# A hybrid convolution and RWKV-7 block: the gate's adaLN rows spread over block 0, the state's update by additions, and split projection weights kept in DRAM

## The chip, the core and the metric

The kernel runs on one core of a Trainium2 chip. The metric is device microseconds (us) from start to end of one execution. Before the change the median of three runs is 3080.32 us (3077.19 to 3084.64).

## What is computed

One decoder block over 2048 tokens of width 1024 with two parallel token mixers and a final RMSNorm. The reference, cut to what matters here:

```python
mod = einsum('bd,de->be', silu(c), ada_w[l]) + ada_b[l]
shift, scale, gate = split(mod, 3, axis=-1)
h = rmsnorm(x, norm_g[l]) * (1 + scale[:, None, :]) + shift[:, None, :]
p = einsum('bsd,de->bse', h, w_in[l])
c_val, c_gate, c_og, ts, r_og, g_conv, g_rwkv = split(p, SPLITS, axis=-1)
y_conv = conv_branch(c_val, c_gate, c_og, ...)      # GLU, causal depthwise conv of width 31, LayerNorm, swish, @ w_conv_out
y_rwkv = rwkv7_branch(ts, r_og, ...)                # 16 heads of 64, per-head norm, SiLU gate, @ w_rwkv_out
m = sigmoid(g_conv) * y_conv + sigmoid(g_rwkv) * y_rwkv
x = x + gate[:, None, :] * (m @ w_out[l])
return rmsnorm(x, final_g)

# in rwkv7_branch, the scan over tokens, per head:
sk = einsum('bhvk,bhk->bhv', state, kk_t)
state = state * w_t[:, :, None, :] - sk[..., None] * b_t[:, :, None, :] + v_t[..., None] * k_t[:, :, None, :]
o_t = einsum('bhvk,bhk->bhv', state, r_t)
```

## The kernel before

**Layout.** Features stand on the 128 partitions, tokens along a row. The tokens are cut into four blocks of 512 (`NB`, `TB`). A matrix product is made of three products of split values, so that it keeps the accuracy of float32: every operand is split in a high part (a cast to `fp32r` on ACT) and a low part (a subtraction). `load_w` brings a 128-column tile of weights (512 KB), casts it on ACT (L175), subtracts on DVE or POOL (L177), and for the input projections writes both parts to DRAM (L181, L182) so that later blocks read them back ready (L168, L169). All weight tiles (`w_st`, `w_hi`, `w_lo`) share six buffers (`WB`): a tile that is loaded and split takes three of them, one that is read back takes two. `mm3` (L192) is a projection: 24 matmuls of 512 columns, or 48 of 256, into a PSUM buffer `ps_main`, of which there are two.

**First phase, blocks 0 to 3** (loop at L859). `hprep` makes the normalised input `h`; in block 0 it also computes shift and scale from 16 of the 24 adaLN rows (`ada_steps`). Then four groups of two pairs of heads. `pair` projects r, k and v, makes the decay factors (`pe` is the decay over a chunk of 64 tokens, one value per feature and chunk), the matrices `KR` and `BK`, the masked products `As` (from copies of `BK` by ACT, `BKz`, L518) and, by eight transposes on PE (L555) and two copies (L556), `tk`, the transposed `BK`. `group` then inverts the triangular blocks of `As` (out to DRAM as `dA`, L595; back as `La`, L600; 62 steps on POOL, L609 and L611; out and back again) and walks through 8 chunks in a chain (L659 to L685): matmuls of `KR` with the state `S`, an addition (L670), matmuls with `As`, a multiplication to `uv` (L675), matmuls of `tk` with `uv`, and the update of the state on DVE, for each of the four heads `S = xo * pe + Se` (L683), where ACT made `Se = S * pe` (L665). `pe` thus multiplies both parts of the new state, chunk by chunk.

Beside the chain PE has input projections to do: those of `conv` (with the 31-tap convolution on DVE, L761) and of `gates`. A tile scheduler puts all of it into one order per engine ahead of time; the order is fixed when the program runs. All DMAs are issued by SP, one after another in its order; a DMA that waits for its data or for a free buffer holds those behind it.

**Rows of the gate.** Behind group 0 of block 0 (L890 to L896) the last eight adaLN rows are read, 512 KB each, in four pairs (`ada_cols`, L206) into buffers of tag `As`, and each is multiplied with the condition's row `srow` and summed on DVE. The result, half the gate, goes to `grow_d` in DRAM. In block 1 `ogate` (L147) multiplies w_o by it, in 16 halves of a tile: load, multiply on POOL, cast on ACT (L157), subtract on POOL (L158), and store both parts (L160). The last phase reads them back.

**Last phase** (from L964, 2446 us in the profile). For each block `rproj` (w_ro) and `cproj` (w_co) project the two mixers' outputs and evict them with the sigmoid gates to `mr` (L962 and L949); the sum is split and goes through w_o (L1059 to L1061); `finish` makes the final RMSNorm of 128 tokens: a few steps on 128x1 (L1074 to L1077 with the reciprocal square root, L125 to L130), two multiplications (L1080) and the stores. In this phase each block loads and splits w_ro and w_co anew, 8 tiles of each: 64 casts (L175) and 64 subtractions on DVE (L177). While one block's w_o is multiplied, the next block's inputs are prepared: `osplit` (L927) and `lnorm` (L984, LayerNorm over the convolution's channels, with `pmean`, `pvar` and `prl` on PE).

## Time and profile before

| what | value |
|---|---|
| time, median of 3 runs | 3080.32 us |
| the profiled execution: its own time | 3079.25 us |
| its span, first to last instruction | 3077.6 us |
| mean granted clock of TensorE | 0.977 |
| PE busy | 2918.8 us, 95% (25672 matmuls) |
| PEld busy (weight loads of PE, beside matmuls) | 2759.5 us, 90% |
| DVE busy | 2182.2 us, 71% |
| POOL busy | 1161.0 us, 38% |
| ACT busy | 1059.7 us, 34% |
| DMA | 638.41 MB, mean 207 GB/s |

Engines: PE is TensorE (PEld its weight loads), DVE VectorE, ACT ScalarE, POOL GpSimd, SP SyncE, which issues the DMAs. A row names the line of the code, the engine, the operation, the tile written and the tiles read. A row of waits gives the time in which the first engine stood idle before that work and what ended the wait. The stages, by where the tiles of each block begin to move: block 0 from 0 to 655 us, block 1 to 1240, block 2 to 1825, block 3 to 2446, the last phase to the end.

### The profile page before, as it was taken

Reading aid. Unit: us, or ns where it says so; the run is one execution under the profiler, and the core shown is the slowest. Engines: PE = TensorE matmul, PEld = TensorE weight load, DVE = VectorE, ACT = ScalarE, POOL = GpSimd, SP = SyncE. Lnnn points to the kernel's source line nnn. Section 1 sums busy time; section 2 is a strip of 40 time slices with the busy share of each in tenths; the row PEclk is TensorE's granted clock in tenths of the full one; section 3 lists DMA queues with packets and bytes.
Section 4 is the critical chain, followed back from the end, with each engine's and each line's share of the span. In section 5 each row is a group of like instructions: output and inputs, shape, how many; then the busy total and the mean of one; then the engine's idle time right before and its main releaser. Section 6 shows DMA issues by size and latency. Waiting matters only on the chain.

```text
span 3077.6 us, 64859 instructions
## 1 busy us (share of the span) xinstructions
PE 2918.8 (95%) x25672; PEld 2759.5 (90%) x25672; DVE 2182.2 (71%) x4199; ACT 1059.7 (34%) x1919; POOL 1161.0 (38%) x1724
## 2 busy tenths in 40 slices
PE   6799998999999999999999999999989999699998
PEld 5789998999999999999999998999989888487888
DVE  7677877787777667777768586867699465877553
ACT  4424444343324241424232323233342224343421
POOL 3355554534343434241323326345445016533100
PEclk9989999999999999999999999999989999799999
DMA  8675767664757586555646567647448658766554
GB/s 301 221 239 192 262 206 268 229 235 136 249 160 229 163 269 218 178 167 173 204 149 217 181 202 247 192 142 224 139 146 263 207 187 287 246 205 220 198 182 161
DMA packets 343327, 638.41 MB, mean 207 GB/s; under 512 B 133424, under 2 KB 152176, under 8 KB 343024
## 3 DMA queue, kind: packets, MB, share of 16 engines
q1 hardware_dynamic: 343024, 634.27, 62.8%
q8 instruction: 202, 3.31, 0.4%
q14 instruction: 101, 0.83, 0.1%
HBM read 462.10 MB, written 170.92 MB: 206 GB/s over the span
## 4 chain that ended last, share of the span: by engine, by line
PE 62%; DVE 12%; DMA 10%; POOL 7%; issue 3%; ACT 2%; SPq 2%; DVEq 0%; POOLq 0%; ACTq 0%
PE ps_main L192 43%; PE aux L524 3%; DVE acc L761 2%; DMA w_st<-w_in_t 2%; POOL TT L611 2%; POOL itmp L609 2%; PE xo L673 2%; PE pout L1061 2%; PE pout L1060 2%; PE pout L1059 2%; DMA w_lo<-kl_in 1%; PE xo L668 1%; DMA w_gr<-grow_d 1%; PE xo L679 1%; PE late L695 1%
## 5 line engine op out<-in xcount | busy, mean ns | idle before, releaser
L192 PE MATMUL ps_main<-h_hi,w_hi 128*128 128x256 f32 x4608 | 961.4, 286 | 20.4 <-ACT w_hi L175 12.2
L192 PE MATMUL ps_main<-h_hi,w_lo 128*128 128x256 f32 x4608 | 962.3, 286 | 13.6 <-POOL w_lo L177 8.0
L192 PE MATMUL ps_main<-h_lo,w_hi 128*128 128x256 f32 x4608 | 956.7, 285 | 0.0
L192 PEld LDWEIGHTS ps_main<-h_hi,w_hi 128*128 128x128 f32 x4608 | 721.7, 190 | 30.4 <-ACT w_hi L175 13.3
L192 PEld LDWEIGHTS ps_main<-h_hi,w_lo 128*128 128x128 f32 x4608 | 719.7, 190 | 21.6 <-POOL w_lo L177 10.0
L192 PEld LDWEIGHTS ps_main<-h_lo,w_hi 128*128 128x128 f32 x4608 | 719.8, 190 | 5.2 <-issue 0.5
L761 DVE SCALAR_TENSOR_TENSOR acc<-u,ck,acc 128x512 f32<-128x512 f32 x928 | 698.6, 753 | 20.0
L175 ACT CAST w_hi<-w_st 128x1024 fp32r<-128x1024 f32 x135 | 141.5, 1048 | 368.9 <-DMA w_st<-w_in_t 151.6
L683 DVE SCALAR_TENSOR_TENSOR S<-xo,pe,Se 64x64 f32<-64x64 f32 x512 | 144.6, 282 | 128.1 <-PE xo L679 118.1
L609 POOL TENSOR_TENSOR itmp<-La,TT 128x126 f32<-128x126 f32 (+22 forms) x496 | 180.7, 364 | 141.9 <-DMA La<-dA 105.9
L611 POOL TENSOR_TENSOR TT<-TT,itmp 128x126 f32<-128x126 f32 (+22 forms) x496 | 190.5, 384 | 37.2
L177 DVE TENSOR_TENSOR w_lo<-w_st,w_hi 128x1024 fp32r<-128x1024 f32 x88 | 119.5, 1359 | 103.7 <-ACT w_hi L175 47.7
L177 POOL TENSOR_TENSOR w_lo<-w_st,w_hi 128x1024 fp32r<-128x1024 f32 x47 | 113.5, 2414 | 134.5 <-ACT w_hi L175 109.0
L665 ACT ACTIVATE Se<-S,pe 128x128 f32<-128x128 f32 x256 | 89.0, 395 | 209.1 <-DVE S L683 208.0
L524 PE MATMUL aux<-KR,BKz 128*128 128x128 f32 x1024 | 138.5, 285 | 13.5 <-ACT BKz L518 8.7
L547 POOL TENSOR_TENSOR vv<-rk,vv 128x512 f32<-128x512 f32 x32 | 44.0, 1374 | 284.2 <-ACT rk L546 268.8
L524 PEld LDWEIGHTS aux<-KR,BKz 128*128 128x128 f32 x1024 | 127.6, 198 | 16.1 <-ACT BKz L518 9.1
L675 DVE TENSOR_TENSOR uv<-xo,rn 64x256 f32<-64x256 f32 x128 | 53.7, 420 | 99.8 <-PE xo L673 98.2
L741 ACT ACTIVATE th<-ps_main 128x512 f32<-128x512 f32 x64 | 38.1, 595 | 210.5 <-PE ps_main L192 157.6
L526 DVE TENSOR_TENSOR As<-aux,maskA 128x512 f32<-128x512 f32 x128 | 87.0, 688 | 27.9 <-PE aux L524 26.4
L451 POOL TENSOR_TENSOR wlo<-wf,wl 64x128 fp32r<-64x128 f32 x64 | 37.4, 584 | 173.6 <-ACT wl L448 171.1
L773 ACT ACTIVATE th<-ps_main 128x512 f32<-128x512 f32 x64 | 38.2, 597 | 184.3 <-PE ps_main L192 179.7
(298 smaller groups left out, 5489.0 us busy)
## 6 DMA issues: line engine op xcount, KB each, us to landing
w_hi<-kh_in SPq DMA_DIRECT2D x219, 512.0 KB, 4.0
w_lo<-kl_in SPq DMA_DIRECT2D x219, 512.0 KB, 5.1
w_st<-w_in_t SPq DMA_DIRECT2D x73, 512.0 KB, 5.0
kh_in<-w_hi SPq DMA_DIRECT2D x71, 512.0 KB, 2.9
kl_in<-w_lo SPq DMA_DIRECT2D x71, 512.0 KB, 4.4
w_st<-w_ro_t SPq DMA_DIRECT2D x32, 512.0 KB, 4.0
w_st<-w_co_t SPq DMA_DIRECT2D x32, 512.0 KB, 3.6
w_hi<-kh_o SPq DMA_DIRECT2D x32, 512.0 KB, 3.7
```

Source lines behind the costliest of these rows:

```text
L175: nc.scalar.copy(hi, st)
L177: lo_eng.tensor_tensor(out=lo, in0=st, in1=hi.bitcast(F32), op=ALU.subtract)
L192: nc.tensor.matmul(ps[:, qs], ww[:, k, :], aa[k][:, qs], start=(k == 0 and t == 0 and q == 0), stop=(k == KT - 1 and t == 2 and q == ms - ...
L524: nc.tensor.matmul(pA[:, c // 2, es], BKz[:, hh, c // 2, es], KR[:, cc, es], start=(c == 0), stop=(c == 3), skip_group_check=True)
L526: nc.vector.tensor_tensor(out=Asb[:, hh, c4 * 4:c4 * 4 + 4, :].rearrange("p (a e) n -> p a (e n)", e=2), in0=pA, in1=flat(maskA).unsqueeze ...
L609: nc.gpsimd.tensor_tensor(out=tmp[:, :ni, :nt], in0=La[:, j:j + 1, j + 1:].broadcast_to([P, ni, nt]), in1=TT[:, :ni, j:j + 1].broadcast_to ...
L611: nc.gpsimd.tensor_tensor(out=TT[:, :ni, j + 1:], in0=TT[:, :ni, j + 1:], in1=tmp[:, :ni, :nt], op=ALU.add)
L665: nc.scalar.mul(Se[:, q, :], Sg[:, q, :], R[q]["pe"][:, c:c + 1])
L673: nc.tensor.matmul(xo[pr_, q, hs], As[q][pr_, hh, c, kcol(e)], XO[pr_, c, q, hs], start=(q == 0 and hh == 0), stop=(q == 1 and hh == 1), s ...
L683: nc.vector.scalar_tensor_tensor(out=Sg[hs, q, hs], in0=xo[hs, 2 + q, hs], scalar=R[q]["pe"][hs, c:c + 1], in1=Se[hs, q, hs], op0=ALU.mult ...
L761: nc.vector.scalar_tensor_tensor(out=acc if i + 1 < HALO else yj, in0=u[:, i:i + TB], scalar=ck[:, j, i:i + 1], in1=acc, op0=ALU.mult, op1 ...
L1059: nc.tensor.matmul(o_, mhi[kk][:, ts_], whi[:, k, :], start=first, stop=False, skip_group_check=True)
```

## The change

Four edits.

1. The condition's row `srow` is stored in DRAM once (`srow_d`). Behind each of block 0's four groups a copy of it is read back to all partitions (512 KB) into a buffer of tag `As`, and one pair of adaLN rows (two of 512 KB) is read and multiplied. The gate's column and `grow_d` are finished behind group 3.
2. `BK` is multiplied by `pe` on POOL (32 times, 128x1024), ahead of the transposes that make `tk`. The state's update is then `S = xo + Se`: two additions for a chunk, each over both pairs of one half of the partitions, where there were four operations.
3. `keep` works in block 2: per group four tiles of w_ro or w_co, in two halves each, are loaded, cast on ACT, subtracted on POOL and stored in DRAM, 32 halves in all (32 casts, 32 subtractions, 64 stores of 256 KB).
4. `load_w` finds these in `kept`, so the last phase reads high and low parts back and splits nothing: 64 casts and 64 subtractions are gone there, and two tiles of 512 KB are read where there was one.

```diff
+    srow_d = dp.tile([D], F32, name="srow_d", tag="srow_d")
...
+    pending = [(name, n) for name in ("ro", "co") for n in range(KT)]
+
+    def keep(name, n, half):
+        back = kept.setdefault((name, n), [dp.tile([P, KT, P], F32R, name=f"k{p_}_{name}{n}", tag=f"k{p_}_{name}{n}")
+                                           for p_ in "hl"])
+        hs = slice(half * 4, half * 4 + 4)
+        st, hi, lo = hx("w_st"), hx("w_hi"), hx("w_lo")
+        nc.sync.dma_start(st.rearrange("p (k n) -> p k n", k=4), wsrc[name][n][:, hs, :])
+        nc.scalar.copy(hi.bitcast(F32R), st)
+        nc.gpsimd.tensor_tensor(out=lo.bitcast(F32R), in0=st, in1=hi, op=ALU.subtract)
+        for d_, s_ in zip(back, (hi, lo)):
+            nc.sync.dma_start(d_[:, hs, :].bitcast(F32), s_.rearrange("p (k n) -> p k n", k=4))
...
+        BKe = BK.rearrange("p a (e n) -> p (a e) n", e=2)
+        nc.gpsimd.tensor_tensor(out=BKe, in0=BKe, in1=pe.unsqueeze(2).broadcast_to([P, NCH, 2 * CH]), op=ALU.mult)
         tk = l3.tile([P, NCH, P], F32, name="tk", tag="tk", bufs=TKB)
...
-            for q, hh in heads:
+            for hh in range(2):
                 hs = slice(64 * hh, 64 * hh + 64)
-                nc.vector.scalar_tensor_tensor(out=Sg[hs, q, hs], in0=xo[hs, 2 + q, hs],
-                                               scalar=R[q]["pe"][hs, c:c + 1], in1=Se[hs, q, hs],
-                                               op0=ALU.mult, op1=ALU.add)
+                nc.vector.tensor_tensor(out=Sg[hs, :, hs], in0=xo[hs, 2:4, hs], in1=Se[hs, :, hs], op=ALU.add)
...
+    nc.sync.dma_start(srow_d.unsqueeze(0), srow[0:1])
...
+            if b == 2:
+                for _ in range(4):
+                    n_ = pending.pop(0)
+                    for half in range(2):
+                        keep(*n_, half)
...
-            if b == 0 and g == GG:
-                for _ in ada_cols(srow, l3, "As", ASB, [((16 + k, 17 + k), (hgate_col[:, k:k + 1], hgate_col[:, k + 1:k + 2]))
-                                                        for k in range(0, KT, 2)]):
+            if b == 0:
+                sr = l3.tile([P, 2, D], F32, name="srow2", tag="As", bufs=ASB)[:, 0, :]
+                nc.sync.dma_start(sr, srow_d.unsqueeze(0).broadcast_to([P, D]))
+                for _ in ada_cols(sr, l3, "As", ASB, [((16 + k, 17 + k), (hgate_col[:, k:k + 1], hgate_col[:, k + 1:k + 2]))
+                                                      for k in (2 * g,)]):
                     pass
...
+                if g == 3:
+                    nc.vector.tensor_tensor(out=hgate_col, in0=hgate_col, in1=ab[:, 16:24], op=ALU.add)
...
+                    nc.sync.dma_start(grow_d.rearrange("(n p) -> p n", p=P), hgate_col)
```

The scheduler makes a new order of it. In the rows below the numbers behind names are buffer numbers, and an "x4" at the end of a row stands for so many such instructions in a row. New line numbers run ahead of the old ones: L225 after is L211 before, L186 is L172, L195 and L196 are L181 and L182, L611 is L595, L616 is L600, L562 is L548, L182 and L183 are L168 and L169.

First, SP behind group 0 of block 0, where the adaLN rows (`ada_st`) are issued among the inverse's transfers (`dA`, `La`) and the next weights (`w_st`). Before:

```order
L211 DMA ada_st<-ada_t 128x1024 x4
L181 DMA kh_in_2025<-w_hi 128x1024
L172 DMA w_st<-w_in_t 128x1024
L211 DMA ada_st<-ada_t 128x1024
L595 DMA dA<-As 32x4x32 x7
L548 DMA bv_d_1_100<-vv 128x512
L595 DMA dA<-As 32x4x32
L211 DMA ada_st<-ada_t 128x1024 x3
L744 DMA co_d_0_195<-th 128x512
L600 DMA La<-dA 64x1024 x2
L774 DMA gr_d_0_259<-th 128x512
L182 DMA kl_in_2026<-w_lo 128x1024
```

And after:

```order
L186 DMA w_st<-w_in_t 128x1024
L196 DMA kl_in_1936<-w_lo 128x1024
L913 DMA srow_1859<-srow_d 128x1024
L225 DMA ada_st<-ada_t 128x1024 x2
L195 DMA kh_in_1997<-w_hi 128x1024
L611 DMA dA<-As 32x4x32 x8
L562 DMA bv_d_1_100<-vv 128x512
L758 DMA co_d_0_195<-th 128x512
L616 DMA La<-dA 64x1024 x2
L196 DMA kl_in_1998<-w_lo 128x1024
L186 DMA w_st<-w_in_t 128x1024
L788 DMA gr_d_0_259<-th 128x512
```

A weight load that stood behind four rows stands ahead of `srow_d` and the two rows now, and the second one behind `La`.

Second, SP in block 2 behind its last group's pairs, where that group's inverse begins. Before:

```order
L595 DMA dA<-As 32x4x32 x8
L548 DMA bv_d_7_122<-vv 128x512
L168 DMA w_hi<-kh_in_7845 128x1024
L600 DMA La<-dA 64x1024 x2
L169 DMA w_lo<-kl_in_7846 128x1024
L168 DMA w_hi<-kh_in_7907 128x1024
L169 DMA w_lo<-kl_in_7908 128x1024
```

And after, where `kh_co` and `kl_co` are the stores of `keep`:

```order
L611 DMA dA<-As 32x4x32
L182 DMA w_hi<-kh_in_7799 128x1024
L183 DMA w_lo<-kl_in_7800 128x1024
L616 DMA La<-dA 64x1024
L174 DMA kh_co_21810<-w_hi 128x512
L170 DMA w_st<-w_co_t 128x512
L174 DMA kl_co_21811<-w_lo 128x512
L616 DMA La<-dA 64x1024
L182 DMA w_hi<-kh_in_7861 128x1024
L183 DMA w_lo<-kl_in_7862 128x1024
L174 DMA kh_co_21810<-w_hi 128x512
L170 DMA w_st<-w_co_t 128x512
```

Loads and stores of `keep` now stand between the two halves of `La` and between the weights read back; in groups 0 and 1 they come in bunches of eight halves, and the last sixteen together here.

Third, DVE in the last phase between block 0's output projection and block 1's first projection, where the final RMSNorm of block 0 meets the eviction of block 1's first PSUM buffer to `mr`. Before:

```order
L1080 SCALAR_TENSOR_TENSOR xt_31907<-xt_31907,rs_32399,fg 128x512
L1080 SCALAR_TENSOR_TENSOR xt_31909<-xt_31909,rs_32399,fg 128x512
L1075 TENSOR_SCALAR vs<-vs 128x1
L130 SCALAR_TENSOR_TENSOR rs_32418<-rs_t,rs_32418 128x1
L1074 TENSOR_REDUCE vs<-sq_31923 128x1
L177 TENSOR_TENSOR w_lo<-w_st,w_hi 128x1024
L202 SCALAR_TENSOR_TENSOR y_31741<-th,y_31741 128x512
L962 SCALAR_TENSOR_TENSOR mr_32472<-rth,ps_main 128x512
```

And after (L1104, L1099, L131, L1098, L986 are L1080, L1075, L130, L1074, L962 of before):

```order
L1104 SCALAR_TENSOR_TENSOR xt_31981<-xt_31981,rs_32473,fg 128x512
L1104 SCALAR_TENSOR_TENSOR xt_31983<-xt_31983,rs_32473,fg 128x512
L1099 TENSOR_SCALAR vs<-vs 128x1
L131 SCALAR_TENSOR_TENSOR rs_32492<-rs_t,rs_32492 128x1
L1098 TENSOR_REDUCE vs<-sq_31997 128x1
L126 TENSOR_SCALAR rs_32511<-vs 128x1
L1104 SCALAR_TENSOR_TENSOR xt_31985<-xt_31985,rs_32492,fg 128x512
L1104 SCALAR_TENSOR_TENSOR xt_31987<-xt_31987,rs_32492,fg 128x512
L1099 TENSOR_SCALAR vs<-vs 128x1
L129 TENSOR_TENSOR rs_t<-rs_32511 128x1
L986 SCALAR_TENSOR_TENSOR mr_32546<-rth,ps_main 128x512
```

The subtraction of a weight (L177) and the LayerNorm's L202 no longer stand ahead of `mr`; the second norm's multiplications do.

More of the change, by code (lines that the diff above doesn't have):

```diff
@@ L889, in hybrid_block @@
             group(b, g, h, lora, fill)
-            if b == 0 and g == GG:
-                for _ in ada_cols(srow, l3, "As", ASB, [((16 + k, 17 + k), (hgate_col[:, k:k + 1], hgate_col[:, k + 1:k + 2]))
-                                                        for k in range(0, KT, 2)]):
-                    pass
-                nc.vector.tensor_tensor(out=hgate_col, in0=hgate_col, in1=ab[:, 16:24], op=ALU.add)
-                nc.vector.tensor_scalar(out=hgate_col, in0=hgate_col, scalar1=0.5, scalar2=None, op0=ALU.mult)
-                nc.sync.dma_start(grow_d.rearrange("(n p) -> p n", p=P), hgate_col)
+            if b == 0:
[3 more added lines that the diff above has]
+                                                      for k in (2 * g,)]):
+                    pass
+                if g == 3:
+                    nc.vector.tensor_tensor(out=hgate_col, in0=hgate_col, in1=ab[:, 16:24], op=ALU.add)
+                    nc.vector.tensor_scalar(out=hgate_col, in0=hgate_col, scalar1=0.5, scalar2=None, op0=ALU.mult)
+                    nc.sync.dma_start(grow_d.rearrange("(n p) -> p n", p=P), hgate_col)
             wcount[0] = WDVE
```

## The prediction

> **What bounds the kernel now.** I read the page first, then the busy time of each engine by stage, then what TensorE (PE) waits for, and last the timeline around its longest waits. These are rows of the busy times by stage; the columns are the stretch, its length, PE busy, PEld, DVE, ACT, POOL, the granted clock, DMA share and GB/s.
>
> ```profile
> 0.00:40.00 40.00, 16.51 (x111) 14.87 (x112) 32.83 (x96) 16.61 (x31) 11.76 (x23) 1.00 0.98 375
> 105.00:200.00 95.00, 83.27 (x710) 80.76 (x709) 60.40 (x92) 26.69 (x39) 47.15 (x82) 0.91 0.73 230
> 200.00:655.00 455.00, 434.80 (x4138) 420.11 (x4138) 348.08 (x642) 180.28 (x303) 229.31 (x304) 0.97 0.69 231
> 655.00:1240.00 585.00, 574.81 (x5625) 558.18 (x5624) 427.68 (x861) 196.75 (x381) 221.51 (x396) 1.00 0.65 207
> 1240.00:1825.00 585.00, 580.65 (x5668) 564.93 (x5666) 424.76 (x866) 193.90 (x372) 183.98 (x365) 1.00 0.56 181
> 2240.00:2320.00 80.00, 71.48 (x625) 67.33 (x624) 76.07 (x133) 32.35 (x55) 38.16 (x34) 0.87 0.48 151
> 2560.00:2700.00 140.00, 105.67 (x532) 88.11 (x533) 101.23 (x157) 51.25 (x92) 91.04 (x64) 0.84 0.75 252
> 2700.00:2900.00 200.00, 191.83 (x1058) 163.66 (x1058) 147.65 (x245) 83.02 (x139) 59.05 (x38) 0.99 0.64 212
> ```
>
> PE does nearly all the time's work: in blocks 1 and 2 (655 to 1825) it idles 10.2 and 4.35 us of 585 each. No part of the change removes a matmul, so time can come only out of PE's idle time and out of slow matmuls after it. The stretch that has both is 2560 to 2700, where the last phase goes from block 0's output projection to block 1's projections: 140 - 105.67 = 34.3 us idle at a clock of 0.84. The start of the kernel is the other. Who ended the idle time in that stretch (us in total, times, longest):
>
> ```profile
> PE ps_main L192 <- DVE rs L125: 10.8, 1, 10.8
> PE ps_main L192 <- ACT w_hi L175: 10.8, 2, 6.2
> PE ps_main L192 <- DVE w_lo L177: 8.5, 3, 4.1
> PE pout L1059 <- DMA w_hi<-kh_o: 3.9, 1, 3.9
> ```
>
> 19.3 us are waits for a weight that ACT and DVE had yet to split. The wait behind "rs L125" is one for a PSUM buffer: PE (third row) goes on when the eviction to `mr` (second) has come through DVE's queue, which is full of the final RMS norm's small steps.
>
> ```profile
> 2609.82 1.23 DVE L130 SCALAR_TENSOR_TENSOR rs<-rs_t,rs 128x1 f32<-128x1 f32 x1
> ...
> 2625.45 0.68 DVE L962 SCALAR_TENSOR_TENSOR mr<-rth,ps_main 128x512 f32<-128x512 f32 x1
> 2626.28 0.77 PE L192 MATMUL ps_main<-m_hi,w_hi 128*128 128x512 f32 x1 [10.81 <-DVE rs L125]
> ```
>
> **Part 1: kept projection weights in the last phase.** It removes 64 casts on ACT and 64 subtractions on DVE between 2446 and 2900 (the subtractions' group, 2400 to 3078: busy us, mean ns, idle time before):
>
> ```profile
> L177 DVE TENSOR_TENSOR w_lo<-w_st,w_hi 128x1024 fp32r<-128x1024 f32 x64 | 87.3, 1366 | 73.7 <-PE ps_main L192 43.5 <-ACT w_hi L175 23.6 <-PE pout L1060 4.9
> ```
>
> So 87 us of DVE go, and on ACT as many casts; and each projection holds two of the six weight buffers instead of three: three are loaded ahead, not two. The 19.3 us go. Of the 10.8 I leave 3: the order shows `mr` still behind two norms, but no 1.2 us subtraction ahead of it, and block 1's LayerNorm has moved two output columns forward, so POOL's work no longer runs beside those norms. The 3.9 us for w_o stay. That is 19.3 + 7.8 = 27 us.
>
> A restart costs more than its wait. Matmuls of 512 columns just after such idle time, and a few us later:
>
> ```profile
> 2447.28 0.63 PE L192 MATMUL ps_main<-o_hi,w_lo 128*128 128x512 f32 x1
> 2447.70 0.63 PE L192 MATMUL ps_main<-o_hi,w_hi 128*128 128x512 f32 x1
> ...
> 2452.12 0.40 PE L192 MATMUL ps_main<-o_hi,w_hi 128*128 128x512 f32 x1
> 2452.36 0.39 PE L192 MATMUL ps_main<-o_lo,w_hi 128*128 128x512 f32 x1
> ```
>
> They start 0.42 us apart, later 0.24. Six such slow starts lose 6 x 0.18 = 1.1 us; I take 1.2 for each of the five waits that end, so 6 us (nothing at the least; at most (0.99 - 0.84) x 140 = 21 us, the clock's whole deficit). The Trainium skill (TensorE: Matmul & The Clock Gate, section on the HAM clock gate) has PE at half rate until it has been busy for about 3.4 us; by that figure each restart loses 1.7 us, an estimate, and the sum below would be 2.5 us lower. The spacing agrees with half rate, 0.42 against 0.24.
>
> Against this I set 3 us for matmuls of the LayerNorm that PE now reaches earlier (its POOL additions may be late there). **2560 to 2700: -30** (bounds: +5 if other waits fill the hole, -48 if all idle and slow time but w_o's goes). After 2700 PE idles 8.2 us, mostly behind norms: **-2** (0 to -8).
>
> **Part 2: the gate's rows.** Before, eight 512 KB rows are read behind group 0 of block 0. DMA issues of SP, then ACT and PE:
>
> ```profile
> 115.20 2.31 SPq L211 DMA_DIRECT2D ada_st<-ada_t  x4
> ...
> 138.05 0.33 SPq L172 DMA_DIRECT2D w_st<-w_in_t  x1
> ```
> ```profile
> 150.86 1.04 ACT L175 CAST w_hi<-w_st 128x1024 fp32r<-128x1024 f32 x1 [11.49 <-DMA w_st<-w_in_t]
> ```
> ```profile
> 151.95 0.79 PE L192 MATMUL ps_main<-h_hi,w_hi 128*128 128x256 f32 x2 [7.28 <-ACT w_hi L175]
> ```
>
> The weight tile issued at 138.05 is cast at 150.86, and PE waits 7.28 us. After, two rows and a copy of the condition row (1.57 MB, not 4.2) stand there, and one weight load moves ahead. I give back 5.5 of the wait and 1 of slow matmuls: **-6.5** (0 to -9). The other three quarters each add 1.57 MB during the inverse of groups 1 to 3. At that stage's 231 GB/s it is 6.8 us of queue; two projections of 24 x 0.24 = 5.7 us are loaded ahead of it: 1 us each, **+3** (0 to +20). Their two multiplications on DVE are old work, moved.
>
> **Part 3: keeping the weights in block 2.** 32 half tiles are loaded, cast on ACT, subtracted on POOL and stored twice, all DMAs on SP. Behind a store that waits for POOL stand the next weight loads, so PE starves if it is held too long. Block 1 does the same in before, with 16 halves and one more POOL step each:
>
> ```profile
> L158 POOL TENSOR_TENSOR w_lo<-w_st,w_hi 128x512 fp32r<-128x512 f32 x16 | 20.7, 1292 | 8.3 <-ACT w_hi L157 8.0
> ```
>
> Block 1 idles 5.9 us longer than block 2. Twice the halves, half the POOL work: **+6** (0 to +18; the last sixteen come in one bunch that runs into an inverse). 25 MB over 585 us lift 181 GB/s to 224, block 1 shows 207.
>
> **Part 4: state's update.** Four scalar_tensor_tensor of 64x64 a chunk become two additions of 64x128:
>
> ```profile
> L683 DVE SCALAR_TENSOR_TENSOR S<-xo,pe,Se 64x64 f32<-64x64 f32 x512 | 144.6, 282 | 128.1 <-PE xo L679 118.1 <-ACT t L419 1.6
> ...
> L675 DVE TENSOR_TENSOR uv<-xo,rn 64x256 f32<-64x256 f32 x128 | 53.7, 420 | 99.8 <-PE xo L673 98.2
> ```
> ```profile
> PE xo L679 <- DVE uv L675: 4.7, 6, 1.5
> ...
> PE xo L673 <- DVE XO L670: 4.0, 4, 1.4
> ...
> PE xo L668 <- DVE S L683: 3.7, 5, 1.1
> ```
>
> One addition lies between 282 and 420 ns; I take 300, nearer to the narrow one: 1.13 us a chunk becomes 0.6, and DVE loses 68 us over 128 chunks. PE waits for the whole chain only 12.4 us, since projections fill it. With DVE freed where it is full (2240 to 2320: 76 of 80 us) I take **-5** (0 to -12).
>
> The price is a multiplication of BK by `pe` on POOL, 32 times, 128x1024. Its bounds are the row below (the same size, also with a broadcast), 1.94 us, and twice POOL's 1.29 us for half the size above, 2.58; I take 1.94, 62 us in all:
>
> ```profile
> L721 POOL TENSOR_TENSOR XO<-XO,grs 128x1024 f32<-128x1024 f32 x16 | 31.1, 1942 | 70.0 <-DVE grs L130 56.4 <-ACT h_hi L351 13.5
> ```
> ```profile
> 704.08 0.62 ACT L518 COPY BKz<-BK 64x512 f32<-64x512 f32 x1 [0.27 <-PE aux L524]
> ```
> ```profile
> 713.47 1.10 PE L555 MATMUL aux<-ident,BK 128*128 128x128 f32 x8
> ```
>
> It stands between the last copy of BK and its transposes; in between POOL idles and 8.8 us pass, so **0** (to +5 without that cover). A rule of the Trainium skill speaks against it: SBUF — State Buffer, section "SBUF: two separate sides", has DVE and POOL share a port pair as an exclusive lock. The 1.23 us of L130 on 128x1 above, beside POOL's work, agree. By it the 62 us and some 41 us of the kept halves also stop DVE: a rival.
>
> **Sum**, against the profiled execution's 3079.25 us (span 3077.6; the median of the runs is 3080.32, 1.1 more): -30 - 2 - 6.5 + 3 + 6 - 5 = -34.5, so **3045 us**.
>
> **Rivals.**
> - *Norms, not weights, hold PE* (chance 0.15). DVE's order has `mr` 0 behind two norms and `mr` 1 behind four; if each small step again takes 1.2 us, PE waits there instead. For it: the 10.8 us are already such a wait. Against: POOL has less to do then. The first term falls to -13: 3062.
> - *DMA takes over* (0.12). 64 times another 0.524 MB over 454 us add 74 GB/s to the 252 and 212 of the rows: 326 and 286. For it: the 3.9 us wait for w_o's landing. Against: 375 in the first 40 us. Both last-phase terms vanish: 3077.
> - *SP is held in block 2* (0.10), the one on the other side. A half holds SP for a landing, a cast and POOL's turn, and weights queue behind. Below a projection's 5.7 us it is hidden; each us more is paid 32 times, and from 5.7 + 40.5 / 32 = 7.0 us the change is slower. At 8 us: 32 x 2.3 = 74, 3113. For it: sixteen halves in one bunch, some between steps of the inverse. Against: block 1's 5.9 us.
> - *The port lock* (0.05): if DVE meets POOL in proportion to its 73% share (428 of 585), 103 us become 75 and eat the 68 saved: no gain from part 4, 5 us more idle, 3055.
>
> **How the numbers follow.** The forecast has 0.58, its own range 3030 to 3058. For 8 in 10 the range takes in the first two rivals and the deeper bounds: 3017 to 3078. Faster by over 0.2% (about what a measurement can tell from no change) is 3074 or less: 0.58 + 0.15 + 0.05 and a third of the DMA case, 0.82. The rest of that case is 0.08 for the same; slower 0.10.
>
> **What would show it.** In 2560 to 2700's counterpart PE has no wait for w_hi or w_lo from ACT or DVE and idles under 15 us. Near 150 the 7.3 us wait is under 2. Block 2 idles under 12 us. The additions take about 0.3 us. The prediction is wrong if idle time after 2560 stays above 25 us behind `mr` or landings, or if block 2 grows by more than 18.

## The result and the profile after

The changed kernel takes 3091.71 us (median of 7 runs, 3088.81 to 3099.0); the kernel before 3080.32 (7 runs, 3077.19 to 3085.61). The ratio is 1.0033, 95% interval 1.0022 to 1.0045: slower by 0.33%, about 10 us. The prediction had 3045 us and a range up to 3078. The profiled execution of the changed kernel is the longest of its seven, 3099.0 us with a span of 3097.3, so some 7 of the 20 us between the two spans are its own, and that of e6, below, lies 16 us under its kernel's median.

To compare, both traces are cut at the same events: at every 128th matmul of the chains (`xo`; a group has 128, so this is within some us of where a group's chain begins), and at the first matmul of each block's output projection (`pout`). Rows of busy times in six stages, with the columns of the prediction's first table; before:

```profile
86.69:291.41 204.72, 180.97 (x1575) 173.35 (x1574) 143.96 (x254) 75.04 (x120) 88.85 (x127) 0.92 0.67 217
621.73:759.20 137.47, 132.93 (x1313) 128.45 (x1312) 104.90 (x212) 52.29 (x96) 45.47 (x69) 1.00 0.57 189
1349.02:1923.87 574.85, 565.36 (x5523) 548.93 (x5521) 409.90 (x828) 188.89 (x360) 200.66 (x364) 0.99 0.61 194
2360.90:2547.80 186.90, 184.17 (x1383) 161.74 (x1382) 107.95 (x194) 50.72 (x81) 20.69 (x14) 0.98 0.62 200
2547.80:2737.74 189.94, 154.93 (x793) 129.61 (x792) 131.68 (x209) 68.47 (x119) 101.81 (x72) 0.88 0.71 240
2737.74:2886.68 148.94, 140.77 (x781) 120.15 (x780) 116.25 (x191) 64.23 (x110) 54.33 (x35) 0.99 0.68 226
```

The same six after:

```profile
86.99:290.28 203.29, 181.23 (x1590) 173.64 (x1589) 134.87 (x225) 75.80 (x122) 98.72 (x135) 0.94 0.63 207
623.36:771.17 147.81, 127.71 (x1231) 122.47 (x1229) 92.98 (x189) 52.15 (x94) 39.46 (x45) 0.93 0.60 178
1362.75:1966.01 603.26, 584.28 (x5634) 566.21 (x5633) 421.70 (x780) 204.64 (x394) 267.36 (x431) 0.99 0.71 232
2398.26:2594.41 196.15, 190.53 (x1419) 167.20 (x1418) 88.47 (x164) 37.37 (x69) 36.84 (x33) 0.98 0.75 257
2594.41:2765.36 170.95, 154.27 (x792) 130.42 (x791) 124.45 (x206) 59.18 (x110) 100.65 (x68) 0.91 0.87 307
2765.36:2904.91 139.55, 138.31 (x782) 118.85 (x781) 77.53 (x159) 39.47 (x81) 40.94 (x30) 1.00 0.81 290
```

The last two rows are the gain that was forecast: 189.94 + 148.94 = 338.9 us became 170.95 + 139.55 = 310.5, 28 us less. The second row is a loss that was not: between the last group of block 0 and the first of block 1 PE idles 147.81 - 127.71 = 20.1 us, where it was 4.5. The third, block 2, idles 19.0 us where it was 9.5. The fourth, the last phase's block 0, has 5.6 in place of 2.7.

Idle time is not the whole of it, since matmuls behind a wait are slow. The next table gives the lost time by stage: for each matmul the distance to the start of the next one, less the median distance of its kind in the kernel before, summed (so it holds waits and slow starts). A stage read from one execution has a spread of its own: five kernels of one PE order up to 1405 us (before, e2, e8, e9 and e10 below) differ by up to 4 us in each stage of block 0 and by 7.5 us in block 1. The last column is a kernel told of below, which does the same work as before in another order.

| stage (cut as above) | before | after | same work, other order (e14) |
|---|---|---|---|
| block 0, groups 0 to 1 | 41.2 | 38.1 | 50.3 |
| block 0, groups 1 to 3 | 27.9 | 33.7 | 42.5 |
| block 0, group 3, to block 1 | 7.8 | 27.9 | 12.4 |
| block 1 | 22.0 | 26.8 | 24.0 |
| block 2 | 23.7 | 38.9 | 23.0 |
| block 3, groups 0 to 3 | 29.2 | 27.5 | 28.4 |
| from there to w_o of block 0 | 7.6 | 12.0 | 10.9 |
| w_o of block 0 to w_o of block 1 | 50.3 | 32.2 | 39.8 |
| to w_o of block 2 | 11.9 | 2.5 | 12.5 |

**The end of block 0.** PE waits twice for a weight there. PE's two matmuls with the longest waits, ACT's casts that ended them, and what SP issued ahead of the two weight tiles, all of the changed kernel:

```profile
651.50 0.79 PE L206 MATMUL ps_main<-h_hi,w_hi 128*128 128x256 f32 x2 [8.39 <-ACT w_hi L189]
...
668.00 0.80 PE L206 MATMUL ps_main<-h_hi,w_hi 128*128 128x256 f32 x2 [6.97 <-ACT w_hi L189]
```
```profile
650.40 1.04 ACT L189 CAST w_hi<-w_st 128x1024 fp32r<-128x1024 f32 x1 [6.66 <-DMA w_st<-w_in_t]
666.90 1.04 ACT L189 CAST w_hi<-w_st 128x1024 fp32r<-128x1024 f32 x1 [15.45 <-DMA w_st<-w_in_t]
```
```profile
638.88 0.38 SPq L913 DMA_DIRECT2D srow<-srow_d  x1
639.35 0.85 SPq L225 DMA_DIRECT2D ada_st<-ada_t  x2
...
641.48 0.44 SPq L186 DMA_DIRECT2D w_st<-w_in_t  x1
```
```profile
651.89 0.41 SPq L920 DMA_DIRECT2D grow_d<-hgate_col  x1
652.39 1.05 SPq L186 DMA_DIRECT2D w_st<-w_in_t  x1
```

The first tile stands behind the condition's row and two adaLN rows (issued at 641.48, cast at 650.40); the second behind the store of the gate's column (652.39 and 666.90). That store writes 1024 pieces of 4 bytes, and the view of its tile gives its time to landing as the longest of all transfers that touch `grow_d`:

```profile
L920 SPq DMA_DIRECT2D grow_d<-hgate_col x1: 407/407/407, 651.9 to 651.9; - x1
...
DMA to landing us min/median/max: 3.8/4.4/13.2
```

In the kernel before the same store stood at 139.68 us, between the weight tile of 138.05 and PE's wait of 7.28 us:

```profile
139.68 0.37 SPq L896 DMA_DIRECT2D grow_d<-hgate_col  x1
```

It landed 12.7 us later, at 152.4. The wait that the prediction put down to the eight rows ended at 151.95. Whether store or rows made it is what one of the experiments asks.

**The last phase.** No wait for `w_hi` or `w_lo` from ACT or DVE is left between the output projections of blocks 0 and 1. What is left there:

```profile
PE pout L1083 <- DVE cth L972: 4.6, 1, 4.6
PE ps_main L206 <- DVE xt L1091: 4.1, 1, 4.1
PE pout L1083 <- DVE xt L1091: 2.9, 1, 2.9
PE pvar L1029 <- POOL qs L1026: 2.7, 1, 2.7
PE pmean L1019 <- POOL ys L1017: 2.6, 1, 2.6
```

### The profile page after: what moved, and what is told of

Read it like the earlier page. It is cut to its first block, busy times and chain, and to the rows that moved or that the text cites. A ratio compares the mean times of both kernels' runs of the same rounds, so it can differ in the third digit from the quotient of the medians.

```text
span 3097.3 us, 64856 instructions
## 1 busy us (share of the span) xinstructions
PE 2933.9 (95%) x25672; PEld 2773.1 (90%) x25672; DVE 2051.7 (66%) x3879; ACT 1009.3 (33%) x1887; POOL 1261.0 (41%) x1788
## 4 chain that ended last, share of the span: by engine, by line
PE 52%; DMA 17%; DVE 11%; POOL 10%; issue 4%; SPq 4%; ACT 2%; POOLq 0%; DVEq 0%; ACTq 0%
PE ps_main L206 35%; POOL TT L627 3%; POOL itmp L625 3%; DMA w_st<-w_in_t 3%; PE aux L538 3%; DVE acc L775 2%; PE xo L689 2%; PE pout L1083 2%; PE pout L1084 2%; PE pout L1085 2%; DMA La<-dA 1%; DMA dT<-TT 1%; DMA xt<-x_in 1%; PE xo L684 1%; DMA w_lo<-kl_in 1%
## 5 line engine op out<-in xcount | busy, mean ns | idle before, releaser
L699 DVE TENSOR_TENSOR S<-xo,Se 64x128 f32<-64x128 f32 x256 | 73.5, 287 | 102.7 <-PE xo L695 99.2
L189 ACT CAST w_hi<-w_st 128x1024 fp32r<-128x1024 f32 x71 | 74.3, 1046 | 184.9 <-DMA w_st<-w_in_t 148.0
L686 DVE TENSOR_TENSOR XO<-xo,XO 128x256 f32<-128x256 f32 x128 | 53.6, 419 | 86.2 <-PE xo L684 66.5
L955 POOL TENSOR_TENSOR ot<-ot,bt 128x512 f32<-128x512 f32 x24 | 34.9, 1456 | 163.5 <-DVE o_lo L936 110.4
```

The lines of the kernel that those rows point to most:

```text
L189: nc.scalar.copy(hi, st)
L699: nc.vector.tensor_tensor(out=Sg[hs, :, hs], in0=xo[hs, 2:4, hs], in1=Se[hs, :, hs], op=ALU.add)
```

## The experiments

Every ratio is against the kernel before on the same chip, whose runs spread over some 10 to 20 us; it is given with its 95% interval. 0.1% is 3.1 us.

### One part at a time

The first kernel has the edit of the adaLN rows alone (the hunks of `srow_d`, `sr` and `if g == 3` of the diff).

> The kernel before with the first edit alone (srow in DRAM, one pair of adaLN rows behind each group of block 0). Theory A (the store of the gate's column, 1024 pieces of 4 bytes, which took 12.7 us to land before and 13.2 us after, holds the weight loads queued behind it wherever it stands, and at the end of block 0 the rows' 1.57 MB add a second wait): slower than before by 12 to 22 us, about 3097, with two waits of 6 to 9 us for w_hi from ACT near 640 to 680. Theory B (these edits are nearly free by themselves, and the waits at the end of block 0 come with the rest of the changed order): within 5 us of before, and no such pair of waits.

Measured: 3096.45 us, 1.0049 (1.0033 to 1.0064), 15 us slower. The trace has waits of 3.5 and 5.5 us at 649 and 664 us (the first is put down to DVE), and 15.8 us of idle time in that stage; the lost time is 27.8 us against 7.8. Both waits are for a weight tile: one stands behind the rows and is cast at 647.59, the other behind the store and is cast at 662.46. The time is theory A's and so is the pair of waits, but they are shorter than the 6 to 9 us that it set. Behind group 0 the lost time falls by 8.7 us (32.5 from 41.2), behind groups 1 and 2 it rises by 5.8.

The second has keep alone (`keep`, `pending` and `if b == 2`).

> The kernel before with keep and the reading back alone. Theory A (the parts add up as the two traces show them stage by stage: about -20 in the last phase, +13 in block 2): faster by 4 to 12 us, about 3072. Theory B (the last phase's gain belongs to keep, and the loss in block 2 to POOL's multiplication of BK by pe, which this kernel doesn't have): faster by 18 to 25 us, about 3059, and block 2 as before.

Measured: 3068.74 us, 0.9961 (0.9946 to 0.9975), 12 us faster. In block 2 the lost time is 38.8 us against 23.7, without any multiplication of BK by pe; so that loss belongs to keep, and theory B falls. PE's order is that of before up to 1405 us.

The third has the state's edit alone (the `BKe` lines and the two additions).

> The kernel before with the multiplication of BK by pe on POOL and the two additions alone. Theory A (the chain was covered by projections, so its shorter steps give nothing that can be measured): within 4 us of before, 3076 to 3084. Theory B (POOL's extra 62 us make its other work, and by it PE, late in blocks 2 and 3): slower by 8 to 15 us. The prediction's own term was 5 us faster.

Measured: 3084.83 us, 1.0019 (1.0005 to 1.0034), 6 us slower by the ratio and 4 by the medians: at the upper edge of theory A or just over it, and under theory B's 8. The group of the additions shows that the instructions cost what the prediction took (300 ns), and DVE lost 71 us of work (144.6 less 73.5 in the changed kernel, which this row is of):

```profile
L699 DVE TENSOR_TENSOR S<-xo,Se 64x128 f32<-64x128 f32 x256 | 73.5, 287 | 102.7 <-PE xo L695 99.2 <-ACT ta L475 1.0
```

The fourth is the kernel before with another way of storing the gate's column.

```diff
-                nc.sync.dma_start(grow_d.rearrange("(n p) -> p n", p=P), hgate_col)
+                pg = pa.tile([P, TB], F32, name="aux", tag="aux")
+                nc.tensor.transpose(pg[0:KT, 0:P], hgate_col, ident)
+                gt = hx("grow")
+                nc.scalar.copy(gt[0:KT, 0:P], pg[0:KT, 0:P])
+                nc.sync.dma_start(grow_d.rearrange("(n p) -> n p", p=P), gt[0:KT, 0:P])
```

> The kernel before, with only the store of the gate's column changed: a transpose on PE and a copy on ACT make it eight rows of 512 bytes, so that the store is 8 pieces, not 1024 of 4 bytes. Theory A (the store held the weight tile that PE waited for at 152 us): the wait of 7.3 us there falls under 3 us, the store lands in 3 to 5 us, and the time falls by 4 to 9 us. Theory B (the wait came from the eight adaLN rows, as the prediction had it): the wait stays at 5 us or more and the time within 3 us.

Measured: 3075.56 us, 0.9986 (0.9971 to 1.0), 4 us faster, at the edge of what the interval tells. SP's order is the same but for the store's neighbours, and the eight rows are where they were. PE's waits between 130 and 200 us are now

```profile
PE ps_main L192 <- POOL w_lo L177: 3.9, 2, 2.8
PE aux L897 <- DVE hgate_col L895: 1.9, 1, 1.9
PE ps_main L192 <- DVE w_lo L177: 0.7, 1, 0.7
```

and none is for `w_hi` from ACT, where 7.28 us stood. The weight tile ahead of the store is cast 6.9 us after its issue; before it was 12.8:

```profile
138.69 0.33 SPq L172 DMA_DIRECT2D w_st<-w_in_t  x1
```
```profile
145.62 1.05 ACT L175 CAST w_hi<-w_st 128x1024 fp32r<-128x1024 f32 x1 [4.61 <-DMA w_st<-w_in_t]
```

So the wait at 152 us was the store's, not the rows': the change didn't remove it but carried it to the end of block 0.

### Parts put together

The changed kernel with that store in eight rows:

> The changed kernel, with the store of the gate's column made eight rows of 512 bytes by a transpose. Theory A (at the end of block 0 one of the two long waits is that store's): the wait of 7.0 us at 668 us goes, that of 8.4 us at 651 us behind the adaLN rows stays, and the time falls by 6 to 12 us against the changed kernel's 3091.7 to 3092: about 3083. Theory B (the rows' bytes alone cause both): no gain, 3089 to 3094.

Measured: 3086.92 us, 1.0024 (1.0013 to 1.0034). PE's waits between 640 and 690 us:

```profile
PE ps_main L206 <- DVE rs_t L130: 8.7, 1, 8.7
PE ps_main L206 <- POOL w_lo L191: 1.2, 1, 1.2
PE ps_main L206 <- DVE h_lo L366: 0.9, 1, 0.9
```

One of the two long waits is gone and the one behind the rows stands (put down to DVE, but its tile was issued at 641.12 behind the condition's row and two adaLN rows and landed at 649.68). That is theory A's mechanism, though the new order also moved the store itself, to 673.84 us, away from the weight tile. The gain against 1.0033 is only 0.09%, 3 us, short of the 6 expected, and it isn't made in this stage: its lost time is 29.8 us, with 27.9 in the changed kernel, since smaller waits, of up to 1.8 us, came in elsewhere in it.

The changed kernel with the rows as before:

> The changed kernel without its first edit: all eight rows behind group 0 of block 0 as before; keep and the state's additions as changed. Theory A (the parts add: -12.2 for keep alone and +3.9 for the state alone): 3069 to 3077, and the end of block 0 without waits over 3 us. Theory B (keep and the state's work on POOL hinder each other in block 2): 3080 or more.

Measured: 3068.88 us, 0.9958 (0.994 to 0.9977), 13 us faster than before: theory A, at its lower edge. In the stage at the end of block 0 PE idles 6.0 us; the longest wait there, 3.8 us, is put down to `XO`, and none is for a weight. Against the whole change (1.0033) the rows' edit costs 0.75%, 23 us. By stages: +1.6 us behind group 0, +6.3 behind groups 1 and 2, +14.9 at the end, 22.8 in all; that this sum meets the 23 us is in part luck, as the spread of a stage is up to 4 us.

Keep, with the store in eight rows:

> The kernel before with keep, and with the gate's column stored as eight rows; neither of the other two edits. If the parts add (-12.2 and -5.4): 3063, 3058 to 3068. If the gain at 152 us is given back later: 3069 or more.

Measured: 3070.18 us, 0.9962 (0.9946 to 0.9978), no better than keep alone. The two gains don't add: on top of e4 (0.9986) keep brings 7 us, not 12, with PE's order that of e4 up to 1397 us; block 2's lost time is the same (38.0), and the stage from there to w_o of block 0 has 18.4 us.

The weights kept at their first use in the last phase, nothing in block 2:

```diff
-KEPT = ("in",)
+KEPT = ("in", "ro", "co")
```

> The kernel before with one word changed: the last phase's block 0 splits w_ro and w_co as before and stores both parts, blocks 1 to 3 read them back; nothing is done in block 2. Theory A (keep's work costs 13 to 15 us in block 2 and brings 29 in the last phase): blocks 0 to 3 as before, 16.8 MB more of stores in the first 110 us of the last phase, and faster than before by 15 to 27 us, 3054 to 3066. Theory B (the stores there delay the weight loads behind them on SP): block 0's projections idle 15 us or more and the time is no better than keep's 3069.

Measured: 3077.16 us, 0.9987 (0.9975 to 0.9999): theory B. Up to the last phase PE's order is that of before, instruction by instruction. From block 3's last group to w_o of block 0 PE idles 18.2 us (2.7 before), and the hole behind it shrinks as with keep (lost time 38.2 + 2.8, from 50.3 + 11.9). Waits of 2.9 and 5.9 us for a weight's split and 2.1 us for w_o's landing stand there now. So the gain is taken back in block 0's part of the last phase; that the stores among its weight loads do it is argued, not shown.

### The price of keep

Keep's work, but the last phase reads none of it (`kept` is filled under another name, so the last phase splits its weights as before):

> The kernel before with keep's work in block 2 (32 halves loaded, cast, subtracted and stored), while the last phase splits its weights as before and reads none of it: the price of keep without its gain. Theory A (about 15 us, from the stages of the kernel with keep alone): slower than before by 8 to 18 us, all of it between 1240 and 1830 us and just behind. Theory B (block 2 pays nothing, and the trace's difference there is chance): within 4 us of before. The prediction's term was +6.

Measured: 3084.58 us, 1.0027 (1.0014 to 1.0039), 8 us slower, with 37.0 us lost in block 2: theory A, at its lower edge. Its order is that of keep alone up to the last phase, so the difference of the two, 0.66% or 20 us, is what the last phase gains.

The same without casts and subtractions:

```diff
-        st, hi, lo = hx("w_st"), hx("w_hi"), hx("w_lo")
+        st = hx("w_st")
...
-        nc.scalar.copy(hi.bitcast(F32R), st)
-        nc.gpsimd.tensor_tensor(out=lo.bitcast(F32R), in0=st, in1=hi, op=ALU.subtract)
-        for d_, s_ in zip(back, (hi, lo)):
+        for d_, s_ in zip(back, (st, st)):
```

> As the kernel with keep unread, but without the 32 casts on ACT and 32 subtractions on POOL: each half is loaded and stored twice as it came (what it stores is never read). Theory A (the price is that SP's queue and the DMA engines are shared): as slow as with them, +8 to +18. Theory B (the price is that ACT and POOL come later with what PE waits for): within 4 us of before.

Measured: 3098.74 us, 1.0065 (1.0051 to 1.0078), 20 us slower, with 48.2 us lost in block 2. Less work took 12 us longer than e9, which neither theory has. ACT and POOL are not needed for the price; but this kernel's order parts from the other's early in block 2, and what an order is worth is the next question.

### The order itself

The state's edit with four operations a chunk, so that only POOL's multiplication is new:

```diff
-            for hh in range(2):
+            for q, hh in heads:
                 hs = slice(64 * hh, 64 * hh + 64)
-                nc.vector.tensor_tensor(out=Sg[hs, :, hs], in0=xo[hs, 2:4, hs], in1=Se[hs, :, hs], op=ALU.add)
+                nc.vector.scalar_tensor_tensor(out=Sg[hs, q, hs], in0=xo[hs, 2 + q, hs],
+                                               scalar=1.0, in1=Se[hs, q, hs],
+                                               op0=ALU.mult, op1=ALU.add)
```

> The kernel before with BK multiplied by pe on POOL, but the state's update still as four scalar_tensor_tensor of 64x64 a chunk, their scalar now 1.0: POOL's price without DVE's saving. Theory A (the additions bring about 5 us and POOL's work costs about 9): slower than before by 6 to 12 us. Theory B (neither matters): within 5 us of before, like the version with additions at +3.9.

Measured: 3119.19 us, 1.0133 (1.0113 to 1.0153), 41 us slower: far outside both.

The changed kernel with no rows behind the last group:

```diff
-                                                      for k in (2 * g,)]):
+                                                      for k in ((0, 2), (4,), (6,))[g]]):
```

(and `if b == 0 and g < 3`, `if g == 2` for the store.)

> The changed kernel, but with the rows of the gate behind groups 0 (two pairs), 1 and 2 (one pair each) of block 0, none behind group 3. Theory A (the loss is at the end of block 0, where rows go ahead of weights that PE waits for): the waits of 7 to 8 us there go, and the time falls by 12 to 22 us against the changed kernel, to about 3074. Theory B (every quarter costs its share, wherever it stands): the time falls by 6 us at most.

Measured: 3108.82 us, 1.0102 (1.0087 to 1.0117). The waits for weights at the end of block 0 are gone (the longest left there is 4.5 us, for `XO` from POOL), as theory A says, and yet the kernel is 21 us slower than the changed one: 45.2 us are lost behind groups 1 and 2, among them a wait of 8.6 us for `w_hi` at 510, and 41.4 in block 1, which this edit doesn't touch.

POOL's multiplication, with ones, in the kernel before:

```diff
+        BKe = BK.rearrange("p a (e n) -> p (a e) n", e=2)
+        nc.gpsimd.tensor_tensor(out=BKe, in0=BKe, in1=pe1.unsqueeze(2).broadcast_to([P, NCH, 2 * CH]), op=ALU.mult)
```

> The kernel before with POOL multiplying BK by a tile of ones, 32 times, ahead of the transposes: the same POOL work at the same place as in the change, while the state's update stays exactly as before. Theory A (POOL's work itself delays what PE waits for): slower by 25 to 45 us. Theory B (it is hidden, and the 41 us of the version with four operations are those of its order): within 12 us of before.

Measured: 3093.62 us, 1.0044 (1.0028 to 1.006), 14 us slower: between the two. Up to 1141 us PE's order is that of before, and block 0 loses 80.3 us, where the five kernels of that order lose 74.0 to 80.9: in that part POOL's multiplication costs nothing that can be told from the spread. The loss comes later, above all between block 3's last group and w_o of block 0 (some 26 us lost, 7.6 before), in another order. The operation itself takes what was estimated, 1.95 us (`pe1`, the tile of ones, is printed as `pe`):

```profile
L553 POOL TENSOR_TENSOR BK<-BK,pe 128x1024 f32<-128x1024 f32 x32 | 62.5, 1953 | 73.7 <-ACT BKz L520 47.2 <-DVE As L528 17.9 <-DVE ss L130 7.4
```

Now the kernel before with two lines' order turned, and no work added or taken. First the copies of BK:

```diff
-            for hh in range(2):
+            for hh in (1, 0):
                 hs = slice(64 * hh, 64 * hh + 64)
                 nc.scalar.copy(BKz[hs, hh], BK[hs, c4 * 2:c4 * 2 + 2])
```

> The kernel before with the two copies of BK (L518) written in the other order, second half of the partitions first: no work is added or taken, but the scheduler makes another order (67% of PE's instructions keep their place). If a remade order by itself moves the time by tens of us: 10 us or more away from before, either way. If not: within 4 us.

Measured: 3096.81 us, 1.0066 (1.0051 to 1.0081), 20 us slower. Its two longest waits in block 0 follow; the first is again for the weight tile beside the store of the gate's column (issued at 141.98, the store at 145.39), and it is 5 us longer than in the kernel before:

```profile
158.96 0.80 PE L192 MATMUL ps_main<-h_hi,w_hi 128*128 128x256 f32 x2 [12.67 <-ACT w_hi L175]
...
554.38 0.77 PE L192 MATMUL ps_main<-h_hi,w_hi 128*128 128x256 f32 x2 [10.82 <-DVE ss L128]
```

Then the state's updates (`for q, hh in heads[::-1]`):

> The kernel before with the state's four updates of a chunk (L683) written in the other order, last head first: no work is added or taken, but the scheduler makes another order (53% of PE's instructions keep their place). If a remade order by itself moves the time by tens of us: 10 us or more away from before, either way. If not: within 4 us.

Measured: 3092.49 us, 1.0054 (1.0039 to 1.0069), 17 us slower. Both are over 10 us away: a remade order by itself moves the time by more than any term of the prediction but one. Of these three orders of the same work that of the kernel before is the fastest. Not every edit gives it up at once: PE's order parts from it at 122 us with the rows' edit (e1), at 217 us with the state's (e3), and with keep only at 1405 us.

### Each part a second time, in the other order

These three have the copies of BK turned as in e14: keep; keep and the state's edit; the whole change.

> The kernel with keep alone, and the two copies of BK swapped as in the second order of the kernel before, which took 3097 beside 3078. Theory A (keep brings 20 us in the last phase and costs 8 in block 2, whatever the order): 12 us faster than that second order, 3079 to 3091. Theory B (an order's chance is larger than keep's gain, also in block 2): 3097 or more, or under 3075.

> Keep and the state's update, the rows of the gate as before, and the two copies of BK swapped. Theory A (the state's edit is worth nothing by itself, only its order moves): within 10 us of the same without the state's edit. Theory B (the state's edit brings 5 us or more): faster than that by 5 or more.

> The changed kernel with the two copies of BK swapped. Theory A (the change's edits together are worth about 0 to -10, and the kernel before had a favourable order that any edit gives up): faster than the second order of the kernel before (3097), 3080 to 3097, with waits for weights at the end of block 0 that add up to 8 us or more. Theory B (the edits themselves cost 10 us or more, in any order): 3105 or more.

Measured: 3095.6 us, 1.0062 (1.005 to 1.0074); 3072.64 us, 0.9995 (0.9983 to 1.0007); 3089.32 us, 1.0047 (1.0034 to 1.006). All ratios to the kernel before:

| edits | first order | copies of BK turned |
|---|---|---|
| none | 1 | 1.0066 |
| keep | 0.9961 | 1.0062 |
| keep and state | 0.9958 | 0.9995 |
| keep, state and rows (the change) | 1.0033 | 1.0047 |

Read downwards: keep brings 12 us and 1 us (e16 has e14's PE order up to 1441 us); the state's edit 1 and 21 (and cost 4 to 6 alone); the rows cost 23 and 16 (and 15 alone). For e16 both theories miss, or nearly: block 2 loses 10 us more than in e14, and the last phase gives 11 back; for e17 theory B holds in this order and A in the other; for e18 theory A. PE's waits for weights at the end of block 0 are back with the rows, in e18 between 640 and 690 us:

```profile
PE ps_main L206 <- ACT w_hi L189: 13.8, 2, 8.8
PE ps_main L206 <- POOL w_lo L191: 2.4, 2, 1.2
```

In that stage the four kernels with a pair of rows behind group 3 idle 15.8 to 20.1 us, the sixteen others 3.7 to 8.5 (8.5 in e12, where the wait is for `XO`).

## Why the prediction was wrong

**The rows of the gate (-6.5 and +3) failed, and they turn the sign:** without them the change is 13 us faster than before (e6), or 2 in the other order (e17). The step was: "two projections of 24 x 0.24 = 5.7 us are loaded ahead of it: 1 us each". They are not: at the end of block 0 the rows stand at SP right ahead of the weight tile that PE needs next. In the changed kernel it is issued at 641.48 and lands 8.8 us later, and the last matmul that needs no new tile starts at 642.72. So no projection covers the queue, and PE waits 8.4 us. The three later quarters lose 26, 21 and 24 us in the three pairs of kernels that differ by this edit alone, and by the order that it remakes (5.8 + 20.0, 6.3 + 14.9, 5.9 + 18.1), not 3. The step before it failed too: the 7.28 us were given to the rows, and e4 shows them to be those of the store at 139.68, which moved along. Behind group 0 the gain is 8.7 us, -1.6 and 1.0 in the three pairs: there the store's wait is gone, and other losses mostly took its place. The store stood in the trace, one row behind the weight tile that the prediction quoted, and it was not priced.

**Keep's gain (-32) was right in mechanism and too large.** All 19.3 us of waits for splits went, and e9 against e2 gives 20 us for the whole last phase by the ratio; the lost time of the two profiles shows 12 of it, and that of e14 and e16, in the second order, 11. By stages of the changed kernel: from block 0's w_o to block 1's the lost time falls by 18.1 us, not 30, since waits of 4.6 and 2.9 us in w_o and 5.3 us for the LayerNorm's sums on POOL came in (3 were allowed). Beyond it falls by 9.4, where 2 were taken; ahead of it 4.4 us are lost, where nothing was set, with the DMA engines at 0.75 of their time in place of 0.62. The 6 us for slow starts did not come: from block 0's w_o to block 1's, lost time less idle time is 15.3 us before (50.3 - 35.0) and 15.5 after (32.2 - 16.7). The wait of 10.8 us behind norms is gone; the one left for a PSUM buffer, behind `xt`, is 4.1. So the first rival (norms hold PE) did not come. Of the second (DMA takes over) the sign is there, 0.87 and 307 GB/s in the hole, and not the loss: its waits for landings are 0.5 us.

**Keep's price (+6)** measured 8 us (e9). The rival on the other side, SP held in block 2 for 8 us a half, did not come: PE idles 19.0 us there, 9.5 more, not 74. What of the 8 us is DMA, and why transfers alone cost 20, stays open.

**The state (-5)** gave +4 to +6 (e3), -1 (e6 against e2) and -21 us (e17 against e16). Instruction times were right (287 ns; POOL's 1.90), DVE's work fell by 71 us, and no gain or loss of its own can be told from the orders. The transposes of BK (L571) wait 3.3 us in all, 1.9 of it for what the profile calls issue and 1.3 for ACT, and e13 agrees: POOL's multiplication was hidden as forecast. The port lock's 75 us did not come, but some of it may have: DVE's busy time fell by 130.5 us (2182.2 to 2051.7), where the additions (71) and the subtractions (87) make 158, so its other work took 28 us longer (the order alone moved it by 8 us the other way, to 2174.2, in e14). With 61 us of the multiplication on POOL and 43 us of keep's subtractions, a DVE operation with both inputs in SBUF took 801 ns where it had 762, 2.5 us in all, and another 1431 where it had 1466. Before, then after:

```profile
L532 DVE TENSOR_TENSOR As<-As,rn 64x512 f32<-64x512 f32 x64 | 48.7, 762 | 2.0
L512 DVE SCALAR_TENSOR_TENSOR rk<-r,hrk,ta 128x512 f32<-128x512 f32 x32 | 46.9, 1466 | 5.3 <-POOL ta L503 5.0
```
```profile
L546 DVE TENSOR_TENSOR As<-As,rn 64x512 f32<-64x512 f32 x64 | 51.2, 801 | 2.0
L526 DVE SCALAR_TENSOR_TENSOR rk<-r,hrk,ta 128x512 f32<-128x512 f32 x32 | 45.8, 1431 | 6.4 <-POOL ta L517 6.2
```

**What the sum left out** is the order. It took each edit as a change to the trace of before, all else in place. But only 37% of PE's instructions keep their position, and two orders of the same work cost 17 and 20 us (e14, e15). Against e14, with the copies turned in both, the whole change is 1.0047 / 1.0066 = 0.9981, 6 us faster, though the two intervals overlap; against the kernel before it is 10 us slower. With the terms as the first order gave them (rows +15 to +23, keep -12, state 0) the prediction's sum would be +3 to +11; but in the second order keep is -1 and the state -21. So of the change's parts the rows' loss of 15 to 23 us and keep's net gain (12 us in the first order, 1 in the second) are shown, and that two other orders of the old work are slower; how much of such a loss stands in the changed kernel, and so a single sum of its +10 us, is not settled. That the 41 us of e11 and the 21 us by which e12 is slower than the changed kernel are orders too is argued, not shown.

Of the signs that it named, the first held for the waits (none for `w_hi` or `w_lo` from ACT or DVE in the hole) and missed its mark for the idle time, 16.7 us where 15 was set. The second held (near 150 us no wait over 1.3), block 2 failed (19.0 us idle, 12 the mark), and the additions took their 0.3 us. Of its signs of being wrong, block 2's growth by more than 18 us came by the stage's length (603.3 from 574.9 us, with 111 more matmuls in it) and not by its lost time (15.2 us more).

Keep alone (e2) and keep with the state's edit (e6) beat both kernels: 12 and 13 us faster than before, 22 and 23 faster than the change.

## What to carry to other kernels

Of a step that is moved, price every transfer by its pieces, not its bytes, and look at what stands next in the queue at the new place: a store of 4 KB held weights for as long as 1.5 MB of rows did. Where a scheduler makes the order anew, first turn two independent lines and measure: here that is 17 to 20 us, and a term below it can't be read from one pair of kernels, only from the same edit in several orders or from its own place in the trace. An order that turned out well is part of what a kernel has, and an edit that remakes it must pay for the loss.

## What the runs showed of the hardware

The store of 1024 pieces of 4 bytes (4 KB) landed after 12.7 us in the kernel before and 13.2 in the changed one, and a weight tile of 512 KB issued 1.6 us ahead of it was cast 12.8 us after its issue; with eight rows of 512 bytes in its place that was 6.9 us. In all 17 kernels that store the column in 4-byte pieces, the weight tile issued within 4 us of the store took 12.2 to 15.8 us to land; in e4 and e7, with eight rows, 6.8 and 8.0 us. The Trainium skill (DMA: Bandwidth & Descriptors, section on rules for kernel authors) has a last dimension that isn't contiguous become one descriptor per element; these traces agree (with the eight rows the profile's page counts 132392 packets under 512 bytes, 1032 fewer than the 133424 before), and add what such a store holds up behind and beside it.

The same update on 64x64 takes 282 ns with its scalar from a column of SBUF (before) and 221 ns with a constant, in the kernel with four operations:

```profile
L685 DVE SCALAR_TENSOR_TENSOR S<-xo,Se 64x64 f32<-64x64 f32 x512 | 113.2, 221 | 110.1 <-PE xo L681 102.0
```
